# Forming the low parts of split weights with accumulating DMAs on GpSimd's queue and ScalarE, in place of a VectorE subtraction

## The chip, the cores and the metric

The kernel runs on one core of one Trainium2 chip. The metric is the device time of one execution in microseconds (us), lower being better. The engines are named as in the profile: PE is TensorE's matmul, PEld its weight load, DVE is VectorE, ACT is ScalarE, POOL is GpSimd, SP is SyncE, which issues the kernel's loads.

## The reference, cut to what matters

A trunk of two layers works on 512 tokens of 1024 features and 256 memory tokens. Each layer has a token mixer (layer 0: an mLSTM, layer 1: a causal pooling mixer), cross attention with four heads into the memory, and an MLP with 4096 hidden features; each is followed by a layer norm. Nearly all of the work lies in products with weights:

```python
proj = x @ w_in                                   # mLSTM: q, k, v, o gate
...
y @ w_out
kv = (mem @ mem_w_kv)
q = (x @ wq)
return o @ wo
return jnp.square(jax.nn.relu(x @ w1 + b1)) @ w2 + b2
```

## The kernel before

Every operand of a matmul is split into two float32r numbers: hi, the value rounded to float32r, and lo, what is left of it. A product is then three matmuls that add up in PSUM (`mm3`: hi by hi, hi by lo, lo by hi).

The weights come in **units** of 128 partitions by 1024 columns of float32 (512 KB), 232 of them in an execution. `unit` loads one into a `raw` tile (a DMA on SP's queue), ScalarE rounds it into `wh` (line 131), and VectorE subtracts `wh` from `raw` and writes `wl` (line 132). There are five buffers for `wh`, five for `wl` and three for `raw`, used in turn; a new unit's `wh` and `wl` go into the buffers of the unit five before it, once the matmuls have read those for the last time.

Units are used in two ways:

- `m_unit` (112 units; w_qk, w_k, w_q, w1): the unit is the stationary operand of one tile of 128 features, 24 matmuls in a row, and is then free. With 512 columns of tokens that is one unit in some 5.4 us.
- `h_units` (120 units in 30 **groups** of four; w_v, w_o, the value half of the memory weights, w_out, w_ao, w2): the four units are the moving operand for half of the output's columns. Each tile of 128 tokens (`token_proj`, 24 matmuls) reads all four in turn, two k tiles from each, so the whole group stays in use until the last token tile. With a group in use one buffer of five is left over.

Groups that follow each other with nothing between them are the second half of the columns after the first, as in `down` (hf = 0, then 1). The fourth MLP quarter of layer 0 (`q == 3`) takes the tokens in two halves of 256 (`z`), and so uses each of its units for 256 tokens and loads them twice.

The order on each engine is set when the program is built, by a scheduler; at run time each engine runs its list in order and waits on semaphores. `defer` and `chain` put small pieces of work (attention scores, transposes) between the matmuls of the large products.

Of the kernel before, what the change touches and what calls it, by code (L numbers as in the profile page):

```python
# [11 lines left out]
AF = mybir.ActivationFunctionType  # L12
ALU = mybir.AluOpType
# [3 lines left out]
D = 1024  # L17
S = 512
# [18 lines left out]
def f32(ap):  # L37
    return ap.bitcast(F32)
# [3 lines left out]
def trunk(ctx: ExitStack, tc: tile.TileContext, a: dict, out: bass.AP):  # L42
    nc = tc.nc
    V, A, G, T = nc.vector, nc.scalar, nc.gpsimd, nc.tensor
# [19 lines left out]
    def ld(dst, src):  # L64
        nc.sync.dma_start(dst, src)

    def const_tile(name, shape):
        t = const.tile(shape, F32, name=name)
        ld(t, a[name])
        return t  # L70

    class Act:
        """hi and lo parts of a feature-major array [1024, S], in two halves of 512 features"""

        def __init__(self, name):
            self.name, self.t = name, {}
# [12 lines left out]
    def t5(name, dt=F32):  # L89
        return t5_p.tile([P, 1280], dt, tag="t5", name=name)  # L90

    def t2(name, n=512, dt=F32):
        return t2_p.tile([P, 512], dt, tag="t2", name=name)[:, :n]

    class ActT:
        """hi and lo parts of a feature-major array [1024, S], in two halves of 256 tokens"""

        def __init__(self, name):
            self.name, self.t = name, {}
# [21 lines left out]
    def unit(src):  # L121
        n = n_units[0]
        n_units[0] += 1
        if n < 5:
            r = xs_p.tile([P, D], F32, tag="xs", name=f"raw{n}")
        else:
            r = raw_p.tile([P, WU], F32, tag="raw", name=f"raw{n}")
        ld(r, src)
        h = wh_p.tile([P, WU], F32R, tag="wh", name=f"wh{n}")
        l = wl_p.tile([P, WU], F32R, tag="wl", name=f"wl{n}")  # L130
        A.copy(h, r)  # L131
        V.tensor_tensor(l, r, f32(h), ALU.subtract)  # L132
        return h, l

    def m_unit(src):
        h, l = unit(src)
        return h.rearrange("p (k m) -> p k m", m=P), l.rearrange("p (k m) -> p k m", m=P)
# [7 lines left out]
    later = []  # L145

    def defer(us, fn):
        """Emit fn after about that much more work for the tensor engine"""
        later.append([us, fn])

    def chain(us, step, fns):
# [15 lines left out]
    def mm3(out_, l, r, start, stop):  # L167
        T.matmul(out_, l[0], r[0], start=start, stop=False)  # L168
        T.matmul(out_, l[0], r[1], start=False, stop=False)  # L169
        T.matmul(out_, l[1], r[0], start=False, stop=stop)  # L170
        if later:
            tick(3 * max(r[0].shape[-1], 128) / 2400)

    def split_psum(d, ps, scale=None):
        dh, dl = d
        if scale is None:
            A.copy(dh, ps)
            V.tensor_tensor(dl, ps, f32(dh), ALU.subtract)
        else:
            A.activation(dh, ps, AF.Copy, scale=scale)  # L180
            V.scalar_tensor_tensor(dl, ps, scale, f32(dh), ALU.mult, ALU.subtract)

    def tok(t):
        return slice(t * P, (t + 1) * P)
# [49 lines left out]
    def token_proj(name, y, w, t, pool_=acc_p, tag="acc", ps=None, ks=range(KC)):  # L234
        if ps is None:
            ps = pool_.tile([P, 512], F32, tag=tag, name=name)
        for k in ks:
            mm3(ps, y.k(k, tok(t)), w[k], start=k == 0, stop=k == KC - 1)
        return ps
# [16 lines left out]
                        defer(LN_T + 0.7 * q, lambda t=t, q=q: transpose_split(x[t], t, dst, [q]))  # L256

    def feat_first(name, n, srcs, x, evac):
        """The first n tiles of 128 features, the first half of the tokens ahead of the second"""
        us = [m_unit(srcs(i)) for i in range(n)]  # L260
        ps = [acc_p.tile([P, 512], F32, tag="acc", name=f"{name}{i}") for i in range(n)]
        for hf in range(2):
            cs = slice(hf * 256, hf * 256 + 256)
            for i in range(n):
                for k in range(KC):
                    mm3(ps[i][:, cs], (us[i][0][:, k], us[i][1][:, k]), x.k(k, cs), start=k == 0, stop=k == KC - 1)
        for i in range(n):
            evac(i, ps[i])
# [5 lines left out]
            mm3(ps, (u[0][:, k], u[1][:, k]), x.k(k, cols), start=k == 0, stop=k == KC - 1)  # L274
        return ps

# [1 line left out]
    zero = t2("zero", 512, F32R)  # L278
    G.memset(f32(zero), 0.0)
    warm = tmp_p.tile([P, 512], F32, tag="tmp", name="warm")  # L280
# [17 lines left out]
    for q in range(4):  # L298
        r = vkv_p.tile([P, 2, 516], F32, tag="vkv", name=f"xr{q}")[:, :, :S]
        for z in range(2):  # L300
            k = 2 * q + z
            ld(r[:, z], a["xT"][:, k])
            h, l = x0.k(k)
# [12 lines left out]
    qk = Act("qk")  # L316

    def qk_k(h):
        """q and k of head h: rows of the halves by pairs of heads"""
        return qk.k(4 * (h // 2) + h % 2), qk.k(4 * (h // 2) + 2 + h % 2)  # L320

    def conv(c):
# [15 lines left out]
    sc = {}  # L338

    def scores(h):  # L340
        """(k q^T) * exp(log weights) of head h, hi and lo, by tiles of keys"""
        ws = {}

        def weights(s):
            n = SEG[s]
            pb = tmp_p.tile([P, 512], F32, tag="tmp", name=f"pb{h}{s}")
            T.matmul(pb[:, :n], sel[:, h], rseg[s], start=True, stop=True)
            gc = gcol[:, s, h : h + 1]
            w = ws[s] = t2(f"w{h}{s}", n)
            V.tensor_scalar(w[:, :P], pb[:, :P], gc, None, op0=ALU.add)  # L350
            G.affine_select(w[:, :P], w[:, :P], pattern=[[1, P]], compare_op=ALU.is_ge, fill=-1e30, base=0, channel_multiplier=-1)
            A.activation(w[:, :P], w[:, :P], AF.Exp)
            if n > P:
                A.activation(w[:, P:], pb[:, P:n], AF.Exp, bias=gc, scale=1.0)

        def part(s):
            if s == 0:
                sc[h] = t5(f"sh{h}", F32R), t5(f"sl{h}", F32R)
            w = ws[s]
            q, k = qk_k(h)  # L360
            n = SEG[s]
            sh, sl = (z[:, OFF[s] : OFF[s] + n] for z in sc[h])
            pS = aux_p.tile([P, 512], F32, tag="aux", name=f"pS{h}{s}")
            mm3(pS[:, :n], (k[0][:, tok(s)], k[1][:, tok(s)]), (q[0][:, s * P :], q[1][:, s * P :]), start=True, stop=True)
            V.tensor_tensor(w, pS[:, :n], w, ALU.mult)
            A.copy(sh, w)
            V.tensor_tensor(sl, w, f32(sh), ALU.subtract)

        fns = []
        for s in range(NT):  # L370
            fns += [lambda s=s: weights(s), lambda s=s: part(s)]
        order = (0, 2, 1, 4, 3, 6, 5, 7)
        return [fns[n] for n in order]

    # v: token-major, with a column of ones for the denominator
    vh = [vkv_p.tile([P, NT, 258], F32R, tag="vkv", name=f"vh{h}") for h in range(H)]
    vl = [vkv_p.tile([P, NT, 258], F32R, tag="vkv", name=f"vl{h}") for h in range(H)]
    for h in range(H):
# [57 lines left out]
    for j, c in enumerate((5, 2, 6, 3, 7, None, None, None)):  # L436
# [3 lines left out]
        ps = token_proj(f"v{hf}{t}", x0, w_v, t)  # L440
        for q in range(2):
            h = 2 * hf + q
# [6 lines left out]
    normg = const_tile("normg", [P, KC])  # L449
    b1 = const_tile("b1", [P, DEPTH, DFF // P])  # L450

    # o gate
    og = [xs_p.tile([P, D], F32, tag="xs", name=f"og{t}") for t in range(NT)]

    def gate(hf, pool_, tag):
# [46 lines left out]
    mk, mv = [], []  # L502

    def mem_k(n):
        """K^T of heads 2n, 2n + 1"""
        t = [vkv_p.tile([P, 1032], F32R, tag="vkv", name=f"k{n}{p}")[:, :1024] for p in "hl"]
        for c in range(4):
            u = m_unit(a["w_k"][4 * n + c])
            ps = aux_p.tile([P, 512], F32, tag="aux", name=f"k{n}{c}")[:, :M]
            for k in range(KC):  # L510
                mm3(ps, (u[0][:, k], u[1][:, k]), (mem[0][:, k], mem[1][:, k]), start=k == 0, stop=k == KC - 1)
            split_psum((t[0][:, c * M : (c + 1) * M], t[1][:, c * M : (c + 1) * M]), ps)
        mk.append(t)
# [19 lines left out]
    for q in range(2):  # L533
        r = raw_p.tile([P, 4, M], F32, tag="raw", name=f"mr{q}")
# [82 lines left out]
        return mixer, new, dst  # L617

    for i in range(DEPTH):
        # cross attention  # L620
        q_ = Act(f"q{i}")

        def evq(c, ps, cs=slice(0, S)):
# [80 lines left out]
        xm = Act(f"xm{i}")  # L704
        out_proj(f"ao{i}", o_, a["w_ao"][i], x, LN(i, 1), xm, (range(4), range(4, KC)))

        # MLP
        ln_load(i, 2)
        ln = LN(i, 2)

        def evh(dst, c, q, ps, n):
            """dst (hi, lo) = relu(ps + b1) ** 2"""
            r = t2(f"r{n}{c}", ps.shape[1])
            A.activation(r, ps, AF.Relu, bias=b1[:, i, 8 * q + c : 8 * q + c + 1], scale=1.0)  # L714
            s = t2(f"s{n}{c}", ps.shape[1])
            V.tensor_tensor(s, r, r, ALU.mult)  # L716
            h, l = dst
            A.activation(h, r, AF.Square)
            V.tensor_tensor(l, s, f32(h), ALU.subtract)
# [13 lines left out]
        for q in range(4):  # L733
            n = f"{i}{q}"
            if q == 3 and i + 1 < DEPTH:
# [4 lines left out]
                for z in range(2):  # L740
# [3 lines left out]
                    tiles = (2 * z, 2 * z + 1)  # L744
# [6 lines left out]
            first = 0  # L751
            if q == 0:
                feat_first(f"h{n}", 4, lambda m: a["w1"][i, m], xm, lambda c, ps: evh(hid.k(c), c, q, ps, n))
                first = 4
# [13 lines left out]
def _layout(inp):  # L768
    c = np.ascontiguousarray

    def feat(w):
        """[D, n * 128] -> [n, 128 (of a k tile), k tile, 128]"""
        k, n = w.shape
        return c(w.reshape(k // P, P, n // P, P).transpose(2, 1, 0, 3)).reshape(n // P, P, -1)

    def half(w):
        """[D, n * 512] -> [n, 4, 128, 2 k tiles * 512]"""
        k, n = w.shape
        return c(w.reshape(4, 2, P, n // 512, 512).transpose(3, 0, 2, 1, 4)).reshape(n // 512, 4, P, 1024)

# [66 lines left out]
```

## Time and profile before

| | |
|---|---|
| time, median of 2 runs | 1245.94 us (1244.35 to 1247.54) |
| span of the profiled execution, first to last instruction | 1242.4 us |
| PE busy | 1231.8 us (99%) |
| DVE busy | 711.6 us (57%) |
| ACT busy | 503.8 us (41%) |
| POOL busy | 8.5 us (1%) |
| DMA, moved / mean | 139.85 MB / 113 GB/s |

For the profiled execution itself the page gives the span alone; the timed runs lie 2 to 5 us above it, their median 3.5 us. The busy times say how full an engine is over the whole span, and not where it waits: the stages of this kernel differ, and an engine with 41% may still be the one that the matmuls wait for in a stage.

### The profile page before, as it was taken

Reading aid. Unit: us, or ns where it says so; the run is one execution under the profiler, and the core shown is the slowest. Engines: PE = TensorE matmul, PEld = TensorE weight load, DVE = VectorE, ACT = ScalarE, POOL = GpSimd, SP = SyncE. Lnnn points to the kernel's source line nnn. Section 1 sums busy time; section 2 is a strip of 40 time slices with the busy share of each in tenths; the row PEclk is TensorE's granted clock in tenths of the full one; section 3 lists DMA queues with packets and bytes.
Section 4 is the critical chain, followed back from the end, with each engine's and each line's share of the span. In section 5 each row is a group of like instructions: output and inputs, shape, how many; then the busy total and the mean of one; then the engine's idle time right before and its main releaser. Section 6 shows DMA issues by size and latency. Waiting matters only on the chain.

```text
span 1242.4 us, 16082 instructions
## 1 busy us (share of the span) xinstructions
PE 1231.8 (99%) x6457; PEld 1053.7 (85%) x6457; DVE 711.6 (57%) x1062; ACT 503.8 (41%) x773; POOL 8.5 (1%) x34
## 2 busy tenths in 40 slices
PE   9999999999999999999999999999999999999997
PEld 6877889889889888888889899998988888888886
DVE  6775466485559534425356889775853442534446
ACT  7576675334423513314235454552351331422420
POOL 0000000000000000000000000000000000000000
PEclk9999999999999999999999999999999999999999
DMA  6232346333323423323336545532332332422411
GB/s 236 64 102 85 103 137 217 119 107 106 98 85 90 131 85 102 102 68 120 118 109 196 169 131 161 170 100 68 103 119 85 107 97 68 131 73 88 133 51 68
DMA packets 41786, 139.85 MB, mean 113 GB/s; under 512 B 5068, under 2 KB 5324, under 8 KB 41712
## 3 DMA queue, kind: packets, MB, share of 16 engines
q1 hardware_dynamic: 41712, 138.84, 35.5%
q8 instruction: 50, 0.82, 0.3%
q14 instruction: 24, 0.20, 0.0%
HBM read 136.72 MB, written 2.10 MB: 112 GB/s over the span
## 4 chain that ended last, share of the span: by engine, by line
PE 94%; DVE 3%; DMA 2%; issue 1%; ACT 0%; SPq 0%; DVEq 0%; ACTq 0%
PE h L169 9%; PE h L168 9%; PE h L170 9%; PE m L170 9%; PE m L168 9%; PE m L169 9%; PE ao L169 2%; PE ao L170 2%; PE ao L168 2%; PE q L169 2%; PE q L170 2%; PE q L168 2%; PE v L168 1%; PE qk L170 1%; PE qk L168 1%; PE v L170 1%
## 5 line engine op out<-in xcount | busy, mean ns | idle before, releaser
L131 ACT CAST wh<-raw 128x1024 fp32r<-128x1024 f32 x232 | 244.3, 1055 | 540.3 <-PE m L170 217.0
L132 DVE TENSOR_TENSOR wl<-raw,wh 128x1024 fp32r<-128x1024 f32 x232 | 283.8, 1224 | 262.7 <-ACT wh L131 257.3
L726 DVE TENSOR_TENSOR xp<-xp,m 128x512 f32<-128x512 f32 x32 | 22.0, 686 | 82.3 <-PE m L170 82.3
L726 DVE TENSOR_TENSOR xin<-xin,m 128x512 f32<-128x512 f32 x32 | 21.9, 686 | 65.9 <-PE m L170 65.9
L168 PE MATMUL h<-xm01h,wh 128*128 128x256 f32 (+1 forms) x176 | 59.0, 335 | 0.0
L168 PE MATMUL h<-xm00h,wh 128*128 128x256 f32 (+1 forms) x176 | 58.5, 333 | 0.0
L170 PE MATMUL h<-xm00h,wl 128*128 128x256 f32 (+1 forms) x176 | 58.4, 332 | 0.0
L170 PE MATMUL h<-xm01h,wl 128*128 128x256 f32 (+1 forms) x176 | 58.3, 331 | 0.0
L169 PE MATMUL h<-xm00l,wh 128*128 128x256 f32 (+1 forms) x176 | 58.3, 331 | 0.0
L169 PE MATMUL h<-xm01l,wh 128*128 128x256 f32 (+1 forms) x176 | 58.3, 331 | 0.0
L168 PE MATMUL h<-xm10h,wh 128*128 128x512 f32 (+1 forms) x144 | 52.8, 367 | 0.0
L168 PE MATMUL h<-xm11h,wh 128*128 128x512 f32 (+1 forms) x144 | 52.8, 367 | 0.0
L169 PE MATMUL h<-xm10l,wh 128*128 128x512 f32 (+1 forms) x144 | 52.6, 366 | 0.0
L170 PE MATMUL h<-xm11h,wl 128*128 128x512 f32 (+1 forms) x144 | 52.6, 365 | 0.0
L170 PE MATMUL h<-xm10h,wl 128*128 128x512 f32 (+1 forms) x144 | 52.6, 365 | 0.0
L169 PE MATMUL h<-xm11l,wh 128*128 128x512 f32 (+1 forms) x144 | 52.6, 365 | 0.0
L714 ACT ACTIVATE r<-h,b 128x512 f32<-128x512 f32 (+1 forms) x72 | 45.6, 634 | 0.3 <-PE h L170 0.2
L716 DVE TENSOR_TENSOR s<-r 128x512 f32<-128x512 f32 (+1 forms) x72 | 45.0, 625 | 0.0
L169 PEld LDWEIGHTS h<-xm00l,wh 128*128 128x128 f32 x176 | 33.4, 190 | 3.2
L168 PEld LDWEIGHTS h<-xm00h,wh 128*128 128x128 f32 x176 | 33.4, 190 | 3.2
L170 PEld LDWEIGHTS h<-xm01h,wl 128*128 128x128 f32 x176 | 33.4, 190 | 3.2
L168 PEld LDWEIGHTS h<-xm01h,wh 128*128 128x128 f32 x176 | 33.4, 190 | 3.1
(594 smaller groups left out, 3268.4 us busy)
## 6 DMA issues: line engine op xcount, KB each, us to landing
raw<-in_w SPq DMA_DIRECT2D x144, 512.0 KB, 3.7
raw<-in_w_q SPq DMA_DIRECT2D x24, 512.0 KB, 4.4
raw<-in_w_ao SPq DMA_DIRECT2D x16, 512.0 KB, 3.7
raw<-in_w_qk SPq DMA_DIRECT2D x8, 512.0 KB, 4.5
raw<-in_w_v SPq DMA_DIRECT2D x8, 512.0 KB, 4.7
raw<-in_w_o SPq DMA_DIRECT2D x8, 512.0 KB, 4.2
raw<-in_w_k SPq DMA_DIRECT2D x8, 512.0 KB, 3.9
raw<-in_w_kvv SPq DMA_DIRECT2D x8, 512.0 KB, 4.7
```

The lines of the kernel that those rows point to most:

```text
L131: A.copy(h, r)
L132: V.tensor_tensor(l, r, f32(h), ALU.subtract)
L168: T.matmul(out_, l[0], r[0], start=start, stop=False)
L169: T.matmul(out_, l[0], r[1], start=False, stop=False)
L170: T.matmul(out_, l[1], r[0], start=False, stop=stop)
L714: A.activation(r, ps, AF.Relu, bias=b1[:, i, 8 * q + c : 8 * q + c + 1], scale=1.0)
L716: V.tensor_tensor(s, r, r, ALU.mult)
L726: V.tensor_tensor(x[t][:, hs], x[t][:, hs], ps, ALU.add)
```

## The change

VectorE no longer takes part in forming `wl`. ScalarE writes the negated weights, rounded to float32r, into `wl` with a second pass over `raw` (line 132 of the changed kernel), and a DMA on GpSimd's queue reads the same 512 KB of weights from DRAM once more and adds them onto the tile (line 133). All lines below these stand one lower than before; the other edits of the diff take comments out.

```diff
         h = wh_p.tile([P, WU], F32R, tag="wh", name=f"wh{n}")
         l = wl_p.tile([P, WU], F32R, tag="wl", name=f"wl{n}")
         A.copy(h, r)
-        V.tensor_tensor(l, r, f32(h), ALU.subtract)
+        A.activation(l, r, AF.Copy, scale=-1.0)
+        G.dma_start(l, src, accum_op=ALU.add)
         return h, l
```

ScalarE's list before, in the first MLP quarter of layer 0, from the last unit ahead of the second half of the columns (76) over the other three units of that half (77 to 79) to the first unit of the next quarter (80); `r007` and `h001h` belong to the MLP's activation:

```order
L131 CAST wh76_4094<-raw76_4092 128x1024
L714 ACTIVATE r007_3958<-h007_3933,b1_1020 128x512
L718 ACTIVATE h001h_3814<-r007_3958 128x512
L131 CAST wh77_4100<-raw77_4098 128x1024
L131 CAST wh78_4106<-raw78_4104 128x1024
L131 CAST wh79_4112<-raw79_4110 128x1024
L131 CAST wh80_4224<-raw80_4222 128x1024
```

The same piece of ScalarE's list in the changed kernel:

```order
L131 CAST wh76_4170<-raw76_4168 128x1024
L715 ACTIVATE r007_4030<-h007_4005,b1_1036 128x512
L132 ACTIVATE wl76_4171<-raw76_4168 128x1024
L719 ACTIVATE h001h_3882<-r007_4030 128x512
L132 ACTIVATE wl77_4178<-raw77_4175 128x1024
L131 CAST wh77_4177<-raw77_4175 128x1024
L131 CAST wh78_4184<-raw78_4182 128x1024
L132 ACTIVATE wl78_4185<-raw78_4182 128x1024
L131 CAST wh79_4191<-raw79_4189 128x1024
L132 ACTIVATE wl79_4192<-raw79_4189 128x1024
L131 CAST wh80_4304<-raw80_4302 128x1024
L132 ACTIVATE wl80_4305<-raw80_4302 128x1024
```

Where ScalarE had one pass for each unit it has two, and for unit 77 the pass for `wl` stands ahead of the one for `wh`.

VectorE's list before, at the same place; line 726 adds a product onto the residual stream:

```order
L726 TENSOR_TENSOR xin2_2114<-xin2_2114,m0002_4040 128x512
L132 TENSOR_TENSOR wl77_4101<-raw77_4098,wh77_4100 128x1024
L132 TENSOR_TENSOR wl78_4107<-raw78_4104,wh78_4106 128x1024
L132 TENSOR_TENSOR wl79_4113<-raw79_4110,wh79_4112 128x1024
L726 TENSOR_TENSOR xin3_2116<-xin3_2116,m0003_4066 128x512
```

GpSimd's list in the changed kernel at that place, which had nothing there before:

```order
L133 DMA wl76_4171<-in_w2 128x1024
L133 DMA wl77_4178<-in_w2 128x1024
L133 DMA wl78_4185<-in_w2 128x1024
L133 DMA wl79_4192<-in_w2 128x1024
L133 DMA wl80_4305<-in_w1 128x1024
```

The three subtractions are gone from VectorE, and each unit has a transfer on GpSimd's queue, in the order of the units, behind ScalarE's pass for the same tile. PE's list has the same 6271 rows, with a few places at which a deferred piece stands a few matmuls earlier or later.

## Rows read from the trace of the kernel before

**Rows 1.** The page: busy times (us, share, instructions); DMA queue (packets, MB, share).

```profile
PE 1231.8 (99%) x6457; PEld 1053.7 (85%) x6457; DVE 711.6 (57%) x1062; ACT 503.8 (41%) x773; POOL 8.5 (1%) x34
...
q1 hardware_dynamic: 41712, 138.84, 35.5%
```

**Rows 2.** Waits of PE: who waited for whom, us in total, times, longest.

```profile
PE warm L282 <- POOL zero L279: 1.3, 1, 1.3
PE pd L588 <- DVE d0l L178: 0.5, 2, 0.3
PE qk L168 <- ACT wh L131: 0.4, 1, 0.4
```

**Rows 3.** Groups of instructions: busy us, mean ns, idle before and its releaser.

```profile
L131 ACT CAST wh<-raw 128x1024 fp32r<-128x1024 f32 x232 | 244.3, 1055 | 540.3 <-PE m L170 217.0
L132 DVE TENSOR_TENSOR wl<-raw,wh 128x1024 fp32r<-128x1024 f32 x232 | 283.8, 1224 | 262.7 <-ACT wh L131 257.3
```

**Rows 4.** Timeline of PE, first MLP quarter, from first to second half (start us, us).

```profile
451.36 0.39 PE L169 MATMUL m<-wl,h000h 128*128 128x512 f32 x1
451.59 0.39 PE L170 MATMUL m<-wh,h000l 128*128 128x512 f32 x1
...
455.89 0.39 PE L168 MATMUL m<-wh,h000h 128*128 128x512 f32 x1
...
457.48 0.39 PE L169 MATMUL m<-wl,h000h 128*128 128x512 f32 x1
...
460.20 0.39 PE L169 MATMUL m<-wl,h001h 128*128 128x512 f32 x1
```

**Rows 5.** Timeline of ACT at the same place, with idle time before and releaser.

```profile
434.11 1.06 ACT L131 CAST wh<-raw 128x1024 fp32r<-128x1024 f32 x1 [3.13 <-PE h L169]
...
452.01 1.06 ACT L131 CAST wh<-raw 128x1024 fp32r<-128x1024 f32 x1 [15.61 <-PE m L170]
453.37 1.06 ACT L131 CAST wh<-raw 128x1024 fp32r<-128x1024 f32 x1 [0.30 <-PE m L170]
454.73 1.06 ACT L131 CAST wh<-raw 128x1024 fp32r<-128x1024 f32 x1 [0.30 <-PE m L170]
```

**Rows 6.** Timeline of DVE at the same place.

```profile
453.10 3.94 DVE L132 TENSOR_TENSOR wl<-raw,wh 128x1024 fp32r<-128x1024 f32 x3 [1.76 <-ACT wh L131]
```

**Rows 7.** The tile raw: issue ns (min/median/max), and us from issue to landing.

```profile
L65 SPq DMA_DIRECT2D raw<-in_w x144: 327/328/791, 354.3 to 1193.3; - x144
...
DMA to landing us min/median/max: 3.3/3.7/7.5
```

**Rows 8.** Windows: us; PE, PEld, DVE, ACT, POOL; PEclk, DMA share, GB/s.

```profile
4.00:8.00 4.00, 3.65 (x8) 1.65 (x6) 1.39 (x2) 2.21 (x3) 0.11 (x1) 1.00 0.99 308
8.00:12.00 4.00, 3.79 (x14) 2.46 (x15) 3.89 (x6) 3.58 (x7) 0.21 (x2) 1.00 1.05 386
12.00:20.00 8.00, 8.00 (x36) 6.47 (x35) 5.46 (x8) 5.40 (x8) 0.11 (x1) 1.00 1.00 397
...
1235.00:1242.40 7.40, 0.00 (x0) 0.00 (x0) 4.10 (x8) 0.29 (x1) 0.00 (x0) 0.81 0.23 87
```

**Rows 9.** Timeline of ACT where w1 units serve 256 tokens (layer 0, fourth quarter).

```profile
657.57 1.05 ACT L131 CAST wh<-raw 128x1024 fp32r<-128x1024 f32 x1
...
660.45 1.05 ACT L131 CAST wh<-raw 128x1024 fp32r<-128x1024 f32 x1 [1.00 <-PE h L169]
...
663.33 1.05 ACT L131 CAST wh<-raw 128x1024 fp32r<-128x1024 f32 x1 [1.00 <-PE h L169]
```

**Rows 10.** Timeline of PE around a w_qk unit between two v tiles.

```profile
49.70 0.39 PE L170 MATMUL qk<-x01h,wl 128*128 128x512 f32 x1
...
56.66 0.39 PE L170 MATMUL qk<-x00h,wl 128*128 128x512 f32 x1
```

**Rows 11.** Timeline of ACT at that place.

```profile
49.90 1.05 ACT L131 CAST wh<-raw 128x1024 fp32r<-128x1024 f32 x1 [0.84 <-PE qk L169]
50.86 0.68 ACT L325 ACTIVATE ac<-qk,convw 128x512 f32<-128x512 f32 x1
```

**Rows 12.** Windows with 170 to 205 and 770 to 800: ACT's line 131 alone (columns as in rows 8).

```profile
170.00:205.00 35.00, 11.56 (x11) 1.00 0.61 195
...
770.00:800.00 30.00, 8.15 (x8) 1.00 0.51 155
```

## The prediction

> **What bounds the kernel now.** I read the busy times first: PE is busy for 1231.8 of 1242.4 us [rows 1]. A busy PE alone says little, so the waits of PE come next: the longest of them is one of 1.3 us at the start, and for weights it waits 0.4 us in all [rows 2]. So PE's matmuls set the time everywhere, and the work on the weights lies wholly beside them. Nothing off PE can be worth more than the 10 us in which PE is idle; for VectorE's 283.8 us on line 132 [rows 3] there is almost nothing to win. The question is whether the new way of forming `wl` still fits behind the matmuls.
>
> That is read where the cover is thinnest, at the step from the first to the second half of the columns. Units 77 to 79 need buffers that the group before still holds. `wl` of its first unit is read for the last time at 451.36 us and is free at 451.75; the second half begins at 455.89; the matmul that needs the new `wl` of unit 77 stands at 457.48, those of units 78 and 79 1.36 us apart behind it, the last at 460.20 [rows 4]. In between, ScalarE's three casts start the moment each buffer is free [rows 5], and VectorE's three subtractions end at 453.10 + 3.94 = 457.04 [rows 6]. So `wl` of unit 79 is ready 3.16 us ahead of its matmul. Whatever takes more than about 3 us longer than the subtraction is seen by PE here.
>
> **The change part by part.** *VectorE* loses 232 x 1.224 = 283.8 us [rows 3]. It releases nobody whom PE waits for, so I put this at zero; at most it returns the 0.5 us that PE waited for VectorE in the pooling mixer [rows 2].
>
> *ScalarE* gains 232 passes over 128x1024. The nearest row is its cast of the same tile, 1.055 us [rows 3]: 245 us, which makes 749 us busy, 60% of the span. It is not the bound on average, but each unit now takes it 2.12 us. At the step above, its list has the pass for wl77 first, then wh77, wh78, wl78, wh79, wl79, at 1.06 us each from 451.8 on: wl77 ends at 452.9, wl78 at 456.0, wl79 at 458.15, later than the subtraction by 1.1 us and still ahead of 460.20. What is queued behind them there is the cast of unit 80, needed only 20 us later.
>
> *The transfers* are what matters. No row shows a transfer issued by GpSimd, nor one that accumulates. The nearest rows are the plain loads of the same 512 KB: 3.3 us at least and 3.7 us at the median from issue to landing, with 0.33 us of issue [rows 7]. What such a load takes of the 16 DMA engines is read where they are full: at a share of 1.00 they move 397 GB/s [rows 8], so 512 KB take 1.32 us. The accumulating transfer must read the weights and also what lies in the tile. The low bound is a plain load (1.32 us of the DMA engines, 3.7 us to landing); the high bound puts its two reads and its write one after the other (3 x 1.32 = 3.96 us, and 3.7 + 2.64 = 6.34 us). I take the middle, two loads: 2.64 us of the DMA engines and 3.7 + 1.32 = 5.02 us to landing. A unit then takes them 1.32 + 2.64 = 3.96 us, for `raw` and `wl` together, since each pass that frees a `raw` tile starts the next load on SP's queue.
>
> The Trainium skill (Collectives: The Full Stack, "The bandwidth ceiling: the fold count and why AG ≠ RS ≠ AR") says that an add inside the DMA engines is slow for its two source reads and not for the add, and gives a measured ratio of 1.93 to a copy; by it the transfer would take 2.55 us, and the sum below would be some 4 us less. No row here shows it.
>
> **The sum.** (a) *Steps into a group.* Unit 77: 452.9 + 5.0 = 457.95, against 457.48. Units 78 and 79 follow at the pace of the DMA engines, 3.96 us each, where PE wants one each 1.36 us: unit 79 lands at 465.9 and PE has waited 5.7 us. Behind it the cover builds up again, since the other three token tiles need no new unit. Of the 30 groups ten come behind something that covers them: the first of w_v, the first halves of w_ao (two), and the first halves of w2 behind w1 units that take 5.4 us each (seven; there the last of the four buffers is free 5.4 us before the group begins and wanted 4.3 us after, 9.7 us for 2.1 us of passes, 0.6 us of the activation between them and 5.0 us of transfer). The other 20 pay: 20 x 5.7 = 114 us.
>
> (b) *Units for 256 tokens.* Those of w1 in the fourth quarter of layer 0 follow each other in 2.88 us [rows 9], against 3.96: 16 x 1.08 = 17 us. The units of w_k and of w_q in layer 1 come slower by their other work (11 in 35 us, 8 in 30 us [rows 12]) and I put them at zero, as I do the units at 5.4 us, which leave 1.5 us of the DMA engines each.
>
> (c) *w_qk between v tiles.* Here a group holds four buffers and each w_qk unit goes through the fifth. Its `wl` was last read at 49.70 and is free at 50.1; the next unit's is wanted at 56.66 [rows 10]. The cast ends at 50.95, an evacuation of 0.68 us stands beside it [rows 11], the negation ends at 52.6, the transfer at 57.7: late by 1.0, five times, 5 us.
>
> (d) *The start.* From 4 to 20 us the DMA engines are full [rows 8]. The first three units add 3 x 2.64 us to that, and PE has nothing else to do; with the first landing some 2 us later than that I take 10 us.
>
> Together 114 + 17 + 5 + 10 = 146 us, a span of 1388 us. The median of the runs lies 3.5 us above the span of the profiled execution, so the time is **1392 us**.
>
> **The rivals.** *The transfer is as cheap as a plain load.* Then a unit takes 2.64 us; unit 79 lands at 452.9 + 3.7 + 5.3 = 461.9 and PE waits 1.7 us: 20 x 1.7 = 34, (b) and (c) nothing, the start 6: **1286 us**. For it speaks that the tile to be added to lies in SBUF.
>
> *The transfer takes three loads' time, or GpSimd's issue as long.* A unit takes 5.28 us; unit 79 lands at 452.9 + 6.3 + 10.6 = 469.8, 9.65 us late: 193 us; (b) 16 x 2.4 = 38, and the 24 units of w_k and w_q, at some 3.5 us each, 43; (c) 11; the start 15: **1546 us**. Beyond 5.4 us a unit nothing would cover it anywhere, and the time would rise by 232 us for each us more.
>
> *PE loses its clock in the waits.* In the stretch behind the last matmul the granted clock is 0.81 on average [rows 8], so it falls when PE stands still; in the span before it was 1.00 throughout. If each of the 20 steps left the 24 matmuls of its first token tile, 5.44 us, at 1.2 GHz instead of 2.4, 109 us came on top: **1501 us**. Against it speaks that the 5.7 us come as three waits of under 3 us with matmuls between them. The Trainium skill (TensorE: Matmul & The Clock Gate, "HAM oscillation — how this bites in real kernels") describes just this, a loop with waits for DMA that falls back to the lower clock again and again; that the trace has no such wait keeps it untested here.
>
> *The landing is hidden after all, so not slower.* If a transfer landed within 460.20 - 458.15 = 2.0 us of its pass, and the DMA engines kept up with three in 4 us, PE would wait nowhere but at the start: **1246 us**. Against it: no load of this size landed in under 3.3 us [rows 7].
>
> **How the numbers follow.** The forecast has 0.45, the cheap transfer 0.20, the dear one 0.18, the clock 0.12, no wait 0.05. The range from 1285 to 1600 leaves out the last, what of the dear case lies above it (some 0.08) and a little below the cheap one. Two per cent, about what a measurement of this kernel can tell from no change, is 25 us: only the last case and none other lies within, so 0.04 for the same, 0.01 for faster, 0.95 for slower.
>
> **What would show it.** Right: PE waits on DMA for `wl` (lines 170 and 171 of the changed kernel), in threes, at the second halves of w2, w_ao and w_out, some 2 to 3 us each; VectorE below 430 us, ScalarE near 750 us; twice the weight bytes moved. The rows of issues give the landing of the new transfers: 5 us for my value, below 4 for the cheap one, above 6 for the dear one; the granted clock beside the waits decides the fourth case. I am wrong if PE's waits are few, or spread evenly over the stages with units of 5.4 us, or if the transfers on GpSimd's queue come at a pace of their own, slower than the 16 DMA engines allow.

## The result, and the profile after

The changed kernel takes 1466.05 us (1465.93 to 1466.17 in 2 runs), 1.1758 times the kernel before, with a 95% interval of 1.1734 to 1.1781. The forecast of 1392 us had the sign and most of the size; the time lies inside the range, 74 us above the forecast. The profiled execution has a span of 1464.2 us, 221.8 us more than before.

The page of the changed kernel, with the busy times, the two large DMA queues and what was read from DRAM (for the first two, compare [rows 1]):

```profile
PE 1312.7 (90%) x6457; PEld 1089.1 (74%) x6457; DVE 449.3 (31%) x830; ACT 703.6 (48%) x1005; POOL 210.7 (14%) x266
...
q0 software_dynamic: 33408, 121.65, 44.3%
q1 hardware_dynamic: 41712, 138.84, 27.5%
...
HBM read 258.36 MB, written 2.10 MB: 178 GB/s over the span
```

PE still has its 6457 matmuls, but is idle for 1464.2 - 1312.7 = 151.5 us where it was idle for 10.6, and busy for 80.9 us more. VectorE lost 262 us and nothing came of it. Of the 258 MB read from DRAM the new queue moves 121.65, in 232 transfers, and it holds 44.3% of the 16 DMA engines' time: 0.443 x 1464.2 / 232 = 2.80 us of them for each.

The groups of the three instructions of a unit (columns as in [rows 3]), and the issues, whose last number is the median of microseconds from issue to landing:

```profile
L132 ACT ACTIVATE wl<-raw 128x1024 fp32r<-128x1024 f32 x232 | 244.8, 1055 | 317.9 <-PE m L170 254.8
L131 ACT CAST wh<-raw 128x1024 fp32r<-128x1024 f32 x232 | 240.3, 1045 | 240.5 <-PE h L170 96.4
...
L133 POOL DMA_DIRECT2D wl<-in_w x144 | 125.6, 872 | 718.4 <-ACT wl L132 294.0
...
raw<-in_w SPq DMA_DIRECT2D x144, 512.0 KB, 8.2
wl<-in_w POOLq DMA_DIRECT2D x144, 512.0 KB, 8.6
```

ScalarE's second pass costs the same as its cast, as assumed. The landing does not: 8.6 us at the median, against the 5.02 that I took. The loads of `raw` land later too, in 8.2 us where they took 3.7 [rows 7].

What PE waits for (columns as in [rows 2]):

```profile
PE m L170 <- DMA wl<-in_w: 60.8, 40, 2.9
PE qk L171 <- DMA wl<-in_w_qk: 14.7, 6, 5.0
PE o L170 <- DMA wl<-in_w_o: 11.5, 4, 6.2
PE h L171 <- DMA wl<-in_w: 9.7, 10, 1.8
PE mo L170 <- DMA wl<-in_w_out: 9.1, 5, 2.7
PE vv L170 <- DMA wl<-in_w_kvv: 8.6, 5, 3.0
PE v L170 <- DMA wl<-in_w_v: 6.5, 3, 3.7
PE ao L170 <- DMA wl<-in_w_ao: 5.5, 2, 2.8
PE q L171 <- DMA wl<-in_w_q: 3.6, 3, 2.6
```

Some 130 us of the 151.5 are waits for `wl`, none of which was there before [rows 2]. They are few and long: 40 in w2, up to 2.9 us each.

The step of [rows 4] in the changed kernel, on PE's timeline (start, length, idle before and its releaser); `h<-xm00h,wh` is the first matmul of the next MLP quarter:

```profile
558.70 0.39 PE L169 MATMUL m<-wh,h000h 128*128 128x512 f32 x1
...
563.25 0.50 PE L170 MATMUL m<-wl,h000h 128*128 128x512 f32 x1 [2.80 <-DMA wl<-in_w]
...
567.77 0.50 PE L170 MATMUL m<-wl,h001h 128*128 128x512 f32 x1 [2.41 <-DMA wl<-in_w]
...
571.41 0.79 PE L170 MATMUL m<-wl,h001h 128*128 128x512 f32 x1 [0.73 <-DMA wl<-in_w]
...
590.08 0.39 PE L169 MATMUL h<-xm00h,wh 128*128 128x512 f32 x1
```

Here are the three waits that the prediction described. The matmul of unit 79 stood 4.31 us behind the start of the second half [rows 4] and now stands 12.71 us behind it, 8.40 us late where 5.7 was forecast. The same place on ScalarE's and on GpSimd's timeline:

```profile
554.59 1.06 ACT L132 ACTIVATE wl<-raw 128x1024 fp32r<-128x1024 f32 x1 [15.61 <-PE m L170]
...
559.34 1.05 ACT L132 ACTIVATE wl<-raw 128x1024 fp32r<-128x1024 f32 x1
```

```profile
556.05 0.86 POOL L133 DMA_DIRECT2D wl<-in_w  x1 [16.31 <-PE m L170]
558.90 0.86 POOL L133 DMA_DIRECT2D wl<-in_w  x1 [1.98 <-PE m L171]
560.79 0.87 POOL L133 DMA_DIRECT2D wl<-in_w  x1 [1.03 <-ACT wl L132]
```

The passes end as forecast: that of unit 77 at 555.65, 102.75 us later than the forecast's 452.9, while the whole place has moved by 558.70 - 455.89 = 102.81 us. GpSimd begins to issue 0.4 us later, and the first tile can be read at 563.25, 7.2 us after that. The other two follow 4.52 and 3.64 us behind it, a pace of 4.1 us where 3.96 was forecast. So the pace was right, and the landing was not.

The same stretch in windows (columns as in [rows 8]):

```profile
563.00:566.00 3.00, 2.11 (x8) 1.42 (x8) 0.00 (x0) 2.01 (x2) 0.12 (x1) 1.00 1.07 279
566.00:570.00 4.00, 2.23 (x7) 1.82 (x8) 0.00 (x0) 0.00 (x0) 0.74 (x1) 0.85 1.05 271
570.00:574.00 4.00, 3.27 (x8) 2.11 (x7) 0.06 (x1) 0.00 (x0) 0.00 (x0) 0.50 1.04 262
574.00:578.00 4.00, 4.00 (x15) 3.17 (x15) 0.63 (x1) 0.00 (x0) 0.00 (x0) 0.79 0.01 2
```

The DMA engines are full from 563 to 574 us and idle behind it. The granted clock falls to 0.50, the 1.2 GHz level, between the second and the third of the three waits, and rises again in the last window.

**Where the 222 us lie.** The n-th weight matmul of the one trace can be set beside the n-th of the other; how much the lag grows across a product is what the change costs there. Between the w_qk units and the v tiles the two lists differ in order, so the border between the first two rows is good to some 2 us.

| place | forecast, us | measured, us |
|---|---|---|
| start and w_qk | 15 | 28.4 |
| the 20 steps | 114 | 151.2 |
| first halves of w2 | 0 | 10.4 |
| w1 (forecast for the units for 256 tokens) | 17 | 14.4 |
| w_k and w_q | 0 | 17.3 |
| sum | 146 | 221.7 |

### The profile page after: what moved, and what is told of

It is laid out like the page before. It is cut to its first block, busy times and chain, and to the rows that moved or that the text cites. A ratio compares the mean times of both kernels' runs of the same rounds, so it can differ in the third digit from the quotient of the medians.

```text
span 1464.2 us, 16356 instructions
## 1 busy us (share of the span) xinstructions
PE 1312.7 (90%) x6457; PEld 1089.1 (74%) x6457; DVE 449.3 (31%) x830; ACT 703.6 (48%) x1005; POOL 210.7 (14%) x266
## 3 DMA queue, kind: packets, MB, share of 16 engines
q0 software_dynamic: 33408, 121.65, 44.3%
## 4 chain that ended last, share of the span: by engine, by line
PE 54%; DMA 21%; issue 18%; POOL 3%; ACT 2%; DVE 1%; POOLq 0%; SPq 0%; DVEq 0%; ACTq 0%
DMA wl<-in_w 12%; PE h L171 7%; PE h L169 7%; PE h L170 7%; PE m L170 7%; PE m L171 6%; PE m L169 6%; POOL wl L133 3%; DMA wl<-in_w_qk 3%; PE q L171 2%; PE q L170 2%; PE q L169 2%; DMA wl<-in_w_o 2%; DMA wl<-in_w_q 1%; PE qk L171 1%
## 5 line engine op out<-in xcount | busy, mean ns | idle before, releaser
L132 ACT ACTIVATE wl<-raw 128x1024 fp32r<-128x1024 f32 x232 | 244.8, 1055 | 317.9 <-PE m L170 254.8
L131 ACT CAST wh<-raw 128x1024 fp32r<-128x1024 f32 x232 | 240.3, 1045 | 240.5 <-PE h L170 96.4
L133 POOL DMA_DIRECT2D wl<-in_w x144 | 125.6, 872 | 718.4 <-ACT wl L132 294.0
L171 PEld LDWEIGHTS h<-xm00h,wl 128*128 128x128 f32 x176 | 33.3, 189 | 13.5 <-DMA wl<-in_w 10.4
L220 ACT ACTIVATE rs<-mv,eps_t 128x1 f32<-128x1 f32 x24 | 7.0, 290 | 66.0 <-DVE mv L218 66.0
L133 POOL DMA_DIRECT2D wl<-in_w_q x24 | 20.9, 872 | 113.1 <-ACT wl L132 45.9
```

Of the source, the lines that this page charges most:

```text
L132: A.activation(l, r, AF.Copy, scale=-1.0)
L133: G.dma_start(l, src, accum_op=ALU.add)
L220: A.activation(rs, mv[:, 1:2], AF.Sqrt, bias=eps_t, scale=1.0)
```

## The experiments

The theory after the result: the transfer costs what its landing and its DMA time say at the few places of thin cover, and nothing elsewhere. The rivals: the clock that PE loses in the waits; the second pass of ScalarE; GpSimd's issue; plain contention of twice the traffic with the loads of `raw`.

**The transfer without the addition.** The DMA overwrites the tile, so `wl` holds the whole weights.

```diff
-        G.dma_start(l, src, accum_op=ALU.add)
+        G.dma_start(l, src)
```

> The transfer on GpSimd's queue stays, with the same waits, but writes the weights plainly instead of adding them (the low parts are then wrong). Theory (the DMA engines are full at the steps into a group, since an added 4 KB row takes them 327 ns against 159 plain, and PE's clock falls in the waits): a row takes about 160 to 190 ns, PE waits some 35 to 60 us for wl instead of 130, the mean granted clock is above 0.98, the time 1285 to 1330 us. Rival (GpSimd's queue itself is slow to land, add or not): landings stay above 7 us, PE's waits above 100 us, the time above 1400 us.

Measured: 1328.7 us in one run, as expected. The row of the new queue and its issues:

```profile
q0 software_dynamic: 33408, 121.65, 27.1%
...
wl<-in_w POOLq DMA_DIRECT2D x144, 512.0 KB, 5.1
```

The same 121.65 MB take 0.271 x 1327.0 / 232 = 1.55 us of the DMA engines each instead of 2.80, and land in 5.1 us instead of 8.6. About 83 of the 220 us come with a second load at all; the other 137 are the price of adding.

**No transfer.** ScalarE's pass stays, VectorE's is gone, and `wl` holds the negated weights.

```diff
         A.activation(l, r, AF.Copy, scale=-1.0)
-        G.dma_start(l, src, accum_op=ALU.add)
```

> The transfer is left out; ScalarE's second pass stays (the low parts are then the negated weights). Theory (all of the loss comes from the transfer): 1240 to 1256 us, as before. Rival (ScalarE's 2.1 us for each unit delay the groups or the activations): PE waits for ScalarE at the steps and the time is 1265 us or more.

Measured: 1247.66 us, ratio 1.0011 (1.0001 to 1.002). The second pass and the loss of VectorE's share together cost nothing and return nothing. Everything is in the transfer.

**Only one kind of unit accumulates.** The unit takes a flag; without it `wl` comes from VectorE as before.

```diff
-        A.activation(l, r, AF.Copy, scale=-1.0)
-        G.dma_start(l, src, accum_op=ALU.add)
+        if acc:
+            A.activation(l, r, AF.Copy, scale=-1.0)
+            G.dma_start(l, src, accum_op=ALU.add)
+        else:
+            V.tensor_tensor(l, r, f32(h), ALU.subtract)
```

With the flag on the 112 feature-tile units alone:

> Only the 112 units of feature tiles (m_unit) use the negation and the accumulating transfer; the 120 units of groups are split with VectorE as before. Theory: the steps into a group cost nothing; what stays are the w_qk units (15 us of waits), the start, and the w1 units for 256 tokens (10 us), with some lost clock: 1265 to 1305 us. Rival (the cost goes with the number of transfers, wherever they are): 112/232 of 220 us, so about 1352 us.

Measured: 1316.4 us, ratio 1.056 (1.0544 to 1.0577), above what was expected, and below the rival's value. PE's waits in it:

```profile
PE qk L174 <- DMA wl<-in_w_qk: 16.7, 5, 4.4
PE h L174 <- DMA wl<-in_w: 12.3, 11, 1.7
PE q L174 <- DMA wl<-in_w_q: 4.7, 2, 2.5
```

By the lag, 31.6 us lie at the start, in w_qk and in the v tiles between its units, 19.8 in w_k and w_q, 19.0 in w1, and none in any group of four units. I had these places too cheap, as in the prediction.

With the flag on the 120 units of the groups alone:

> The other half: only the 120 units of groups (h_units) use the accumulating transfer. Theory: nearly all of the loss stays, since it sits at the steps into a group: 1400 to 1445 us, with PE waiting for wl in threes. Rival (by the number of transfers): 120/232 of 220 us, about 1360 us.

Measured: 1404.8 us in one run, as expected, 159 above the kernel before. The two halves add up: 70 + 159 = 229, against 220 for both together. Its largest row of waits is nearly that of the changed kernel, where w2 has 60.8 us:

```profile
PE m L173 <- DMA wl<-in_w: 62.5, 38, 3.4
```

**Only the 56 units of w1 that serve 512 tokens,** which PE takes 5.4 us each to use.

> Only the 56 units of w1 that serve 512 tokens, one in 5.4 us, use the negation and the accumulating transfer; all others are split with VectorE. Theory (a transfer costs nothing where its unit has some 20 us and the DMA engines are full a good half of the time): 1243 to 1256 us. Rival (each transfer costs its 0.95 us wherever it is, as the sum of the two halves suggests): 1299 us.

Measured: 1250.46 us, ratio 1.0029 (1.0019 to 1.0038), as expected. All that PE waits for `wl` in it:

```profile
PE h L174 <- DMA wl<-in_w: 3.8, 2, 2.3
```

Both waits stand at the third unit of a layer's MLP: PE takes the first four units there in two halves of 256 columns, so that they are wanted faster than one in 5.4 us. At the other units it waits for none.

The transfers land no sooner there, in 8.7 us at the median (6.1 to 10.6); with 5.4 us a unit and buffers ahead that is covered. They come in bursts, behind each step into a group, and in a burst the DMA engines are full (columns as in [rows 8]):

```profile
573.50:596.20 22.70, 22.70 (x102) 18.80 (x101) 6.68 (x9) 13.58 (x17) 3.48 (x4) 1.00 1.05 275
```

For 40 of the 56 transfers they are full from issue to landing, and these 40 were issued while the transfer before was still under way; they land in 9.0 us at the median, the other 16 in 7.4. So this run does not show what a landing takes beside idle DMA engines; it shows that a landing of this length costs nothing at the units that PE takes 5.4 us each to use. This is the best version with the transfer in it; none beat the kernel before.

**The clock held up.** Matmuls of a zero tile, which add nothing to the result, stand ahead of the matmuls that wait at the 20 steps: 9, 9 and 3 of them.

```diff
+    def keep(ps, w, k):
+        for n in range({2: 9, 4: 9, 6: 3}.get(k, 0)):
+            T.matmul(ps[:32], zw, w[0][0], start=False, stop=False)
...
         for k in ks:
+            if fill:
+                keep(ps, w, k)
             mm3(ps, y.k(k, tok(t)), w[k], start=k == 0, stop=k == KC - 1)
```

> The changed kernel with 420 idle matmuls of 512 columns (95 us of PE's time in all; they add zero to the sum that is being formed) at the 20 steps into a group: 9 each ahead of the second and third unit and 3 ahead of the fourth, where PE waited 2.8, 2.4 and 0.7 us. Theory (PE's busy time grew by 81 us because the clock falls in the waits): the fillers take the place of waits, PE's waits for the units of groups fall from 102 us to under 40, the time at 1.2 GHz from 150 us to under 80, and the whole is faster than the changed kernel in spite of more work: 1415 to 1445 us. Rival (the clock is not what lengthened it, or the fillers come on top): 1466 us or more, up to 1560.

Missed: 1484.06 us, ratio 1.1895 (1.1874 to 1.1916), slower than the change itself by 18 us. The clock did come up: by the trace the low level lasts for 60 us instead of 155. At the step shown above, on PE's timeline:

```profile
569.87 2.25 PE L151 MATMUL m<-wh,zw 128*32 128x512 f32 x9
...
573.28 0.50 PE L177 MATMUL m<-wl,h000h 128*128 128x512 f32 x1 [0.92 <-DMA wl<-in_w]
...
581.15 0.51 PE L177 MATMUL m<-wl,h001h 128*128 128x512 f32 x1 [1.25 <-DMA wl<-in_w]
```

The half begins at 568.51 here, so its last wait ends 12.64 us behind the start, against 12.71 without the fillers. PE runs at full clock and is busy, and still the fourth unit sets the end. By the lag, 8 of the 17 us that this run loses on the changed kernel lie at one step, the one into the second half of w_v (15.8 us against 7.6); the rest is spread over the others.

**Fewer of them,** 5 and 5, so that the fillers themselves stand less in the way:

```diff
-        for n in range({2: 9, 4: 9, 6: 3}.get(k, 0)):
+        for n in range({2: 5, 4: 5}.get(k, 0)):
```

> The fillers once more at half the size: 200 idle matmuls, 5 ahead of the second and of the third unit of the 20 groups, 47 us of PE's time in all, well inside the waits. Theory now (a step lasts until the fourth unit's transfer has landed; matmuls at 1.2 GHz between the waits only eat up waiting, so the lower clock costs little of its own): PE's waits shrink by about the fillers, 1445 to 1470 us. Rival (the lower clock is a loss of its own, 81 us of longer matmuls): 1425 us or less.

Measured: 1479.85 us, ratio 1.1884 (1.186 to 1.1907), with 75 us at the low level. Missed by a little, on the slow side; the rival of the clock is out by more than 50 us.

**The tile to add from SBUF.** The transfer reads the `raw` tile in place of DRAM.

```diff
-        G.dma_start(l, src, accum_op=ALU.add)
+        G.dma_start(l, r, accum_op=ALU.add)
```

> The accumulating transfer reads the weights from the raw tile in SBUF and not from DRAM again. Theory (a row takes double for its two reads through one engine, whatever they come from): 320 to 330 ns a row, and no gain: 1430 to 1520 us, the raw tile being held longer. Rival (the second reading of DRAM is what costs): rows under 250 ns and under 1400 us.

Measured: 1467.2 us in one run, as expected, with these rows:

```profile
q0 software_dynamic: 33408, 121.65, 43.4%
...
HBM read 136.72 MB, written 2.10 MB: 95 GB/s over the span
...
wl<-raw POOLq DMA_DIRECT2D x232, 512.0 KB, 6.0
```

DRAM gives half the bytes and the transfer holds the DMA engines as long: in the trace's packets a row of 4096 bytes takes 328 ns from SBUF and 327 from DRAM at the median, where a plain one takes 159 on SP's queue and 174 on GpSimd's. So the price is not in reading DRAM a second time; it comes with the add, wherever the operand lies. That the landing falls to 6.0 us and the time does not follow has a reason that the trace shows: the transfer now holds `raw` until it has landed, and the next load waits for that buffer. SP's queue waits for the transfer 223 times, and ScalarE's casts of w1 and w2 wait 194.9 us for `raw`, where they wait 69.5 in the changed kernel:

```profile
SPq L65 <- DMA wl<-raw: 1240.1, 223, 26.2
...
ACT wh L131 <- DMA raw<-in_w: 194.9, 69, 8.2
```

By the lag, the second halves of w2 for 512 tokens that another product follows pay 4.8 to 6.5 us instead of 7.3 to 9.6, and w_q of layer 1 pays 21.8 instead of 5.9.

**The traffic with nobody waiting.** VectorE forms `wl` as before; the same 232 transfers go into a spare tile that nobody reads, one behind the other. There was room for that tile only with two `raw` buffers in place of three, so a second kernel has the two buffers alone.

```diff
-    raw_p = pool("raw", 3)
+    raw_p = pool("raw", 2)
...
         V.tensor_tensor(l, r, f32(h), ALU.subtract)
+        G.dma_start(spare, src, accum_op=ALU.add)
```

> The kernel before, with VectorE's subtraction, and beside it the same 232 accumulating transfers on GpSimd's queue into one spare tile that nobody reads, each waiting only for the one before it; to make room there are two raw buffers and not three (the control has that alone). Theory (waiting for wl is the loss, not the traffic): a transfer lands in about 6 to 7 us, all 232 are through before the end, and the time is within 20 us of the control. Rival (the traffic as such delays PE through the raw loads): 60 us or more above the control.

> The kernel before with two raw buffers in place of three, as the control for the run with unused transfers. Both theories: no transfer on GpSimd's queue; the loads have one tile less of lead, so 1246 to 1290 us.

Measured: 1572.8 us with the transfers, 1274.0 us without them. The expectation on the first is missed by far, and the trace shows two reasons that have nothing to do with the question. All its waits, and its last stretch (columns as in [rows 8]):

```profile
POOL spare L135 <- DMA spare<-in_w: 837.1, 143, 8.6
...
ACT w L355 <- POOL w L354: 125.4, 12, 36.5
...
PE qk L171 <- DVE w L368: 34.5, 1, 34.5
```

```profile
1425.00:1570.00 145.00, 4.66 (x21) 3.54 (x19) 8.08 (x15) 0.59 (x2) 20.90 (x24) 0.52 0.57 98
```

The transfers into one tile follow each other and outlast PE's work by some 145 us, and GpSimd, which waits for each of them, keeps the mixer waiting for a few operations that are also its own (line 354). What can still be read is the MLP of layer 0, where GpSimd has no other work. Across its first three quarters the lag behind the kernel before grows by 4.6 us here and by 1.2 us in the control, where the changed kernel's grows by 32. The traffic alone, with nobody waiting for it, costs some 3 us there. In the fourth quarter, whose units serve 256 tokens, it grows by 32 us here against 8 in the control and 45 in the changed kernel: where units are wanted fast the traffic alone costs time too. In the whole run ScalarE's casts of w1 and w2 wait 191.3 us for `raw`, in the control 109.4. These runs have two `raw` buffers, so how much of that the changed kernel pays with its three is not shown.

## Why the prediction was right, and where its size was wrong

**What bounds the kernel, and what is free.** Right. Without the transfer the time is that of before, so VectorE's 284 us and ScalarE's second pass together are worth nothing. VectorE at 449 us missed my "below 430"; ScalarE has 704 where I said near 750.

**The DMA time of a transfer.** Right in kind and nearly in size: 2.80 us of the DMA engines against 2.64 forecast, 1.8 times the plain transfer on the same queue (1.55), and a pace of 4.1 us a unit against 3.96. The Trainium skill (Collectives: The Full Stack, "The bandwidth ceiling: the fold count and why AG ≠ RS ≠ AR") gives a ratio of 1.93 between a ring's AllGather, which copies, and its ReduceScatter, which adds inside the DMA engines, and puts it down to the add's two source reads. The packets here agree: 327 / 174 = 1.88 against a plain row on the same queue, 327 / 159 = 2.06 against one on SP's; and the transfer from SBUF pays as much. With the 2.55 us that the prediction sets beside its own 2.64, its sum comes out lower by some 7 us, not by 4: 0.27 us at each of 20 steps, 0.09 at each of 16 units, and under 1 us in (c) and (d).

**The landing.** This is the step that failed. "I take the middle, two loads: 2.64 us of the DMA engines and 3.7 + 1.32 = 5.02 us to landing" took the landing of a plain load on SP's queue and added only DMA time. The plain transfer on GpSimd's queue already lands in 5.1 us rather than 3.7 (SP's loads beside it in 4.7), and the accumulating one in 8.6 at the median and 7.2 at the step shown. In the trace's packets these 7.2 us are 1.6 from issue to the first row, 5.1 from the first row to the last, and 0.5 to the landing; while the rows move, loads of `raw` hold 5.5 of the 16 DMA engines at the mean. The forecast counted those loads in the pace of the units and left them out of the landing. Put into the same sum, unit 79 is 2.2 us later by the landing, 0.4 by the time from pass to issue and 0.2 by the pace: 8.4 us late instead of 5.7.

**The sum over the steps.** The term "20 x 5.7 = 114 us" measured 151.2, 7.6 us a step. At the steps where the clock cost nothing it is 7.3: the last wait ends some 8.1 us late there, and about 0.8 us of the next token tile's matmuls are done before it ends. The seven first halves of w2, put at zero because 9.7 us were there for 7.7 us of work, pay about 1 us each and one of them 4.1: with 8.6 us of landing that cover is just too short. Of the 4.1 us, 2.1 are a wait and most of the rest is matmuls at the low clock behind it. The first halves of w_ao pay nothing, as said.

**The small units.** The 16 units of w1 for 256 tokens paid 11.0 us against 17, right in kind. The other 3.4 us of w1 lie almost wholly at the first four units of each layer's MLP, which PE takes in halves and which I put at zero. w_k and w_q: 17.3 against zero. Of these, 13.0 us were wrong by my own numbers, since [rows 12] give 3.2 and 3.75 us a unit, below the 3.96 of the forecast; "slower by their other work" was not enough. The other 4.3 lie at the first four units of w_q in layer 0, which are taken in halves too. The units at 5.4 us cost nothing, shown by the run with w1 alone. Start and w_qk have the landing in them too: 13 and 15 us against 10 and 5.

**The rival of the clock.** Its mechanism is there, its price mostly not. The low level lasts 155 us in the changed kernel, and PE's busy time grew by 81 us. But between two waits a slow matmul only takes the place of waiting. That can be seen without any experiment in the windows of the second halves of w2 for 512 tokens, from the first matmul to the end (columns as in [rows 8]):

```profile
558.70:590.00 31.30, 25.36 (x97) 19.59 (x96) 2.75 (x4) 7.72 (x9) 3.47 (x4) 0.89 0.55 135
656.30:685.20 28.90, 24.06 (x97) 18.68 (x96) 2.75 (x4) 7.64 (x9) 3.51 (x4) 0.94 0.59 146
754.70:783.60 28.90, 23.70 (x97) 18.32 (x96) 7.61 (x10) 9.65 (x11) 3.48 (x4) 0.94 0.73 183
1142.10:1173.30 31.20, 25.34 (x97) 19.48 (x97) 2.75 (x4) 7.69 (x9) 3.49 (x4) 0.89 0.55 134
1239.80:1268.80 29.00, 23.91 (x97) 18.49 (x96) 2.75 (x4) 7.62 (x9) 3.49 (x4) 0.94 0.56 143
1335.40:1364.30 28.90, 23.98 (x97) 18.51 (x96) 2.76 (x4) 7.64 (x9) 3.49 (x4) 0.94 0.60 146
```

In all of them the last wait ends 12.3 to 12.7 us behind the start. Where the clock fell and rose again before that (0.94), the half takes 28.9 or 29.0 us; where it fell late, as in the windows of the step above, some ten matmuls behind the last wait run at 0.43 us instead of 0.23, and the half takes 31.2 to 31.3. So the clock is worth 2.3 us at two of these six steps and nothing measurable at the others, not the 5.44 us at each of 20 that the rival set. With fillers and a clock of 1.00, the first of them takes 30.3 us: less than 31.3 and more than 28.9, because the fillers themselves are in the way. That is why holding the clock up won nothing. At other places more of the low level lies behind a last wait. By the trace's record of the clock, the matmuls at the low level take some 64 us longer in all than they would at the high one; 40 us of that have no wait for `wl` in the 3 us that follow them, and 24 us none in the 12 us that follow. So the clock's part of the 222 us is, as an estimate from these figures, 24 to 40 us; no run here separates it, since the fillers cost PE's time too.

**Why 8.6 us.** The trace's packets tell most of it. In the changed kernel 41 of the 232 transfers found GpSimd's queue idle; at the median their rows begin 1.6 us behind the issue, and they land in 7.2 us; the other 191 were issued while the one before was under way, their rows begin, at the median, just as the other's last row ends, and they land in 8.9. From its first row to its last a transfer takes 4.1 us at the median, though it needs only 2.80 us of the 16 DMA engines, since the loads of `raw` move beside it; a plain one takes 2.4. Into the spare tile, where each transfer waits for the one before, it landed in 5.9 us.

**Open.** What makes up the 1.6 us between issue and first row, and what a landing takes with no load beside it, was not separated. More buffers for `wl`, which would lengthen the cover, were not tried: beside three `raw` buffers there is no room for another.

## What to carry to other kernels

Work that moves from an engine to a DMA is to be measured against the shortest time from the release of a buffer to its next use, not against idle shares: here 57% busy on VectorE was free, and 8 us of landing were seen at 20 steps and hidden behind 5.4 us units. Take the landing of a new kind of transfer, on its own queue, as an unknown with an upper end well above a plain load's, since what was too small here was the delay and not the bandwidth; and count in it whatever else moves beside it, or ahead of it on its queue. A low clock between waits for the same group of transfers cost nothing measurable here; look for it behind the last wait.

## What the runs showed of the hardware

- An accumulating DMA row of 4096 bytes takes 327 ns, with the other operand in DRAM or in SBUF alike (327 and 328); a plain one takes 174 on the same queue and 159 on SP's (medians).
- An accumulating transfer issued by GpSimd occupies GpSimd for 0.87 us and a plain one for 0.53. The plain one lands in 5.1 us, where SP's loads land in 4.7 in the same run and in 3.7 before the change [rows 7].
- On GpSimd's queue the accumulating transfers went one behind the other: 191 of 232 were issued while the one before was under way, and at the median the rows of one began just as the last row of the other ended. The landing was 7.2 us at the median when the queue was idle, 8.9 when it was not, and 5.9 when each transfer waited for the one before.
- The granted clock fell to 0.50 within one step with three waits of under 3 us and matmuls in between; before the change it did so only behind the last matmul [rows 8].
